# Modulation dots cut into pieces and begun at the gate tiles, and a bank of their own for the opening's idle products

## The chip, the cores and the metric

One core of one Trainium2 chip runs the whole kernel. The metric is device time in microseconds (us) of one execution; lower is better. TensorE (PE) multiplies into PSUM, its weight loads are shown as PEld; VectorE (DVE) and ScalarE (ACT) do the elementwise work; GpSimd (POOL) and SyncE (SP) mostly issue transfers here.

## The reference

Two layers, each over x of 512 tokens by 1024 features. A vector c of 1024 numbers steers each layer through six modulation vectors:

```
c_act = silu(c)
mod = c_act @ w_ada + b_ada                 # 1024 -> 6 * 1024
sh1, sc1, g1, sh2, sc2, g2 = split(mod, 6)
h = rmsnorm(x, norm1_w) * (1 + sc1) + sh1
u = h @ w_in                                # pool, conv, q, k, v and three gates per feature
merged = sum over the three mixers of sigmoid(gate_i) * (mixer_i @ p_i)
x = x + g1 * (merged @ w_out)
h2 = rmsnorm(x, norm2_w) * (1 + sc2) + sh2
x = x + g2 * ((silu(h2 @ w_gate) * (h2 @ w_up)) @ w_down)
```

The third mixer is block-sparse causal attention with eight heads of 64. All values are fp32.

## The kernel before

Activations lie with features on the 128 partitions and the 512 tokens along the free dimension, in eight tiles. Each fp32 product is made of three products of rounded halves (`mm3`, line 155): high by high, high by low, low by high. Weights come in tiles of eight 128x128 blocks. `load_w` fetches one into a buffer of the tag `raw`, of which there are three, and splits it: ScalarE copies the high half (`whi`), and the low half (`wlo`) is made either by VectorE (line 402) or, for most input columns and for the attention tiles, by ScalarE and an accumulating transfer (lines 419, 421 and 423). `next_w` hands them out in order and loads three or four ahead.

The modulation vectors are not computed on TensorE. For each of the six parts and each of its eight tiles of 128 features, `ada_load` fetches 128 rows of the transposed w_ada, and `ada_dot` (line 479) multiplies them by silu(c), laid out on all partitions as `csil`, and sums along the free dimension: one VectorE instruction over 128x1024 that leaves one column of `mod`. `ada_end` adds the bias and, for a scale, folds in the norm's weight.

These dots are spread between the products by a queue, `bulk`. `mm3` counts columns, and every 2048 of them (four calls, twelve products) is a tick. A tick steps the attention's generators and gives the queue a credit, `bulk_rate`. As long as the credit is not negative the next task is emitted and its cost subtracted. Unused credit is kept up to 4.0, and `flush_bulk` emits all that is left. Emission sets the place in the program; VectorE's dots keep that order.

In layer 0 the parts are placed so. The first scale and shift (`SC1`, `SH1`) are computed in the opening with the first norm. The second scale (`SC2`) is queued when the attention has begun, with `early` set: its tiles use the `raw` buffers, since the others are in use by the attention, and the load of the next tile is emitted ahead of each dot. The first gate (`G1`) and the second shift (`SH2`) follow at the first attention tile of the merge, the step `("attn", 0)` of the list `GATE2`, and the second gate (`G2`) at the output projection:

```
if l == 0:
    bulk.extend(ada_tasks(l, (SC2,), True))
bulk_rate[0] = 0.0
ahead_now[0] = 3
ready.append(gate())
...
    if j == 2:
        bulk_rate[0] = 0.25
```

Here the merge of pool and convolution branches runs over j, two gate tiles and four products for each, while the attention of four head pairs runs in between. Then come the third gate and the attention branch by `GATE2`, and the output projection in `tail`, which flushes the queue ahead of its sixth column and prepares the second norm.

In the opening, the squares of x are summed over the features by products with two columns of ones, into bank 0 of the two-bank tile `scratch`. Products of `ones` by `ones`, which nobody reads, go to bank 1 (`idle`): three of them after the sums and five after the root of the norm has been spread by four transposes. Each is two MATMULs in the trace. The root is read from bank 0 by ScalarE (line 920).

Of the kernel before, what the change touches and what calls it, by code (L numbers as in the profile page):

```python
# [17 lines left out]
ALU = mybir.AluOpType  # L18
AX = mybir.AxisListType
PSUM = bass.MemoryType.PSUM  # L20

P = 128
D = 1024
S = 512
L = 2
KT = D // P
# [37 lines left out]
SH1, SC1, G1, SH2, SC2, G2 = range(6)  # L64
# [9 lines left out]

WARM = 9

WARM2 = (3, 5)

GATE2 = ([("gate", j) for j in range(6)] + [("attn", 0), ("attn", 1), ("gate", 6), ("gate", 7)]
         + [("attn", j) for j in range(2, 8)])  # L80
# [3 lines left out]
def hybrid_trunk(ctx, tc, xT, ws, ada, cols, pool_w, qk_w, crow, pos, con, out):  # L84
    nc = tc.nc
    V, A, T = nc.vector, nc.scalar, nc.tensor
# [10 lines left out]
    def nm(s):  # L97
        uid[0] += 1
        return f"{s}{uid[0]}"
# [7 lines left out]
    def ps_mm():  # L107
        return psum.tile([P, S], F32, tag="mm", name=nm("mm"), bufs=4)

    def ps_pair():  # L110
        return psum.tile([P, 2, S], F32, tag="pair", name=nm("pair"), bufs=2)

    def w4(shape, dt=F32):
        return work.tile(shape, dt, tag="w4", name=nm("w4"), bufs=6)

    def sm(shape, dt=F32, tag="sm", bufs=8):
        return small.tile(shape, dt, tag=tag, name=nm(tag), bufs=bufs)
# [7 lines left out]
    bulk = deque()  # L125
    bulk_rate, credit = [0.0], [0.0]
# [8 lines left out]
    def flush_bulk():  # L135
        while bulk:
            bulk.popleft()[1]()
# [12 lines left out]
    def drain():  # L150
        while fibers:
            tick()

    def matmul(*a, **k):
        tc.keep_in_program_order(T.matmul(*a, **k))  # L155

    def pin(ins):
        return tc.keep_in_program_order(ins)

    def transpose(*a):  # L160
        tc.keep_in_program_order(T.transpose(*a))  # L161
# [28 lines left out]
    csil = const.tile([P, D], F32, name="csil")  # L190

    c8, ccol = sm([KT, P], tag="c8", bufs=1), sm([P, KT], tag="ccol", bufs=1)
# [13 lines left out]
    ones = f32(ones_r)  # L206
# [70 lines left out]
    class GateUp:  # L277
# [9 lines left out]
        def load(self, sub):  # L287
            if sub < 2:
                return self.pair[sub].first()
            if sub < 6:  # L290
                return self.pair[sub % 2].sums(sub // 2 - 1)
            raw = rawt()
            fetch(raw, self.l, self.pair[0].blocks(1, 1) + self.pair[1].blocks(1, 1))
            return split_w(raw, C_BLOCKS)
# [159 lines left out]
    def next_w(ahead=None):  # L454
        ahead = ahead_now[0] if ahead is None else ahead
        while at[0] < len(items) and len(loaded) <= ahead:
            loaded.append(load_w())
        return loaded.popleft()

    def wblk(w, b):  # L460
        return w[0][:, b, :], w[1][:, b, :]
# [6 lines left out]
    mod = [const.tile([P, 6, KT], F32, name=f"mod{l}") for l in range(L)]  # L468
    amod = [[const.tile([P, KT], F32, name=f"am{l}{i}") for i in range(2)] for l in range(L)]

    def fold_scale(l, i, j0, j1):
        part = SC1 if i == 0 else SC2
        nw = colt[:, l, (C_N1 if i == 0 else C_N2) + j0:(C_N1 if i == 0 else C_N2) + j1]
        V.scalar_tensor_tensor(amod[l][i][:, j0:j1], mod[l][:, part, j0:j1], 1.0, nw,
                               op0=ALU.add, op1=ALU.mult)
# [9 lines left out]
    def ada_first_load(j, after=None, parts=(SC1, SH1)):  # L485
        tiles = {}
        for part in parts:
            tiles[part] = w4([P, D])
            with issued_after(after):
                nc.sync.dma_start(tiles[part], ada[0, part, j])  # L490
        return tiles
# [7 lines left out]
    def ada_first(j, tiles, part):  # L499
        first_dots[j, part] = pin(ada_dot(tiles[part], 0, part, j))  # L500
        m = mod[0][:, part, j:j + 1]
        if part == SC1:
            ins = A.activation(amod[0][0][:, j:j + 1], m, AF.Identity, scale=minus[:, j:j + 1],
                               bias=abias[:, j:j + 1])
        else:
            ins = A.activation(m, m, AF.Identity, bias=colt[:, 0, C_ADA + part * KT + j:C_ADA + part * KT + j + 1])
        if j == 0:

            pin(ins)
        return ins  # L510

    def ada_load(l, part, j, early, kept):
        aw = wp.tile([P, D], F32, tag="raw", name=nm("raw"), bufs=RAW) if early else w4([P, D])
        nc.sync.dma_start(aw, ada[l, part, j])
        kept.append(aw)

    def ada_step(l, part, j, kept):
        aw = kept.pop(0)
        with tc.issue_after(dots_after[0].ins) if dots_after[0] is not None else nullcontext():
            ins = ada_dot(aw, l, part, j)  # L520
        pin(ins)

    def ada_end(l, part):
        m = mod[l][:, part]
        V.tensor_add(m, m, colt[:, l, C_ADA + part * KT:C_ADA + (part + 1) * KT])
        if part in (SC1, SC2):
            fold_scale(l, 0 if part == SC1 else 1, 0, KT)
        if part == G1:
            V.tensor_scalar(m, m, 0.5, None, op0=ALU.mult)

    def ada_tasks(l, parts, early=False):
        every = [(part, j) for part in parts for j in range(KT)]
        kept, out = [], []
        load = lambda n: ada_load(l, *every[n], early, kept)

        def step(n):
            if early and n + 1 < len(every):
                load(n + 1)
            if not early:
                load(n)  # L540
            ada_step(l, *every[n], kept)

        if early:
            out.append((1.2, lambda: load(0)))
        for n, (part, j) in enumerate(every):
            out.append((1.2, lambda n=n: step(n)))
            if j == KT - 1:
                out.append((0.2, lambda part=part: ada_end(l, part)))
        return out
# [323 lines left out]
    scratch = ps_pair()  # L873
# [3 lines left out]
    for i in range(WARM):  # L877
# [4 lines left out]
        if i == 6:  # L882
            for j in range(KT):
# [4 lines left out]
    step = []  # L888
    pin(V.tensor_scalar(minus, colt[:, 0, C_N1:C_N1 + KT], -1.0, None, op0=ALU.mult))
    pin(V.scalar_tensor_tensor(abias, colt[:, 0, C_ADA + SC1 * KT:C_ADA + (SC1 + 1) * KT], 1.0,  # L890
                               minus, op0=ALU.add, op1=ALU.mult))
# [3 lines left out]
    def sum_tokens(t):  # L895
# [2 lines left out]
                   start=not groups and i == 0, stop=len(groups) == KT // 2 - 1, skip_group_check=True)  # L898
        groups.append(t)

    def idle(n):
        for _ in range(n):
            matmul(scratch[:, 1, :P], ones, ones, start=True, stop=True)

    for k in range(KT):
        if k == 0 or (k % 2 == 1 and k < KT - 1):
# [9 lines left out]
    first[0].update(ada_first_load(0, step[3], (SH1,)))  # L916
    idle(WARM2[0])
    ss = scratch[:, 0, :2 * TT].rearrange("p (t c) -> p t c", c=2)[:, :, 0]
# [7 lines left out]
    for i in range(TT):  # L926
        transpose(norm.rstd[:, i * P:(i + 1) * P], r[:, i:i + 1].to_broadcast([P, P]), ident)
    idle(WARM2[1])
    ada_first(0, first[0], SH1)
    norm.first_scaled(0)  # L930
# [21 lines left out]
    for l in range(L):  # L952
# [230 lines left out]
        for t, src in keys_values(qk, ss, made, tables, turn):  # L1183
            for half in range(2):
                part = src[:, half * BLOCK:(half + 1) * BLOCK].rearrange("p (n d) -> p n d", d=HD)
# [5 lines left out]
        def gate():  # L1191
            g = ps_mm()
            feature_tile(g, next_w())
            sg = bigt(F32)
            A.activation(sg, g, AF.Tanh, scale=0.5)
            return sg
# [18 lines left out]
            y_pool.append(split_from(pp, scale=col(C_PS + j)))  # L1215

        if l == 0:
            bulk.extend(ada_tasks(l, (SC2,), True))
        bulk_rate[0] = 0.0
        ahead_now[0] = 3  # L1220
        ready.append(gate())

        def gated(sg, branch):

            V.scalar_tensor_tensor(sg, sg, 1.0, branch, op0=ALU.add, op1=ALU.mult)

        pcw = None
        for j in range(KT):
            s0, s1 = [ready.pop(0) if ready else gate() for _ in range(2)]
            if j == 2:  # L1230
                bulk_rate[0] = 0.25
            if j % 2 == 0:
                pcw = next_w()
            b0 = 4 * (j % 2)
            p1, p2 = ps_mm(), ps_mm()
            for z in range(2):
                mm3(p1, wblk(pcw, b0 + z), y_pool[z], z == 0, z == 1)
            for z in range(2):
                mm3(p2, wblk(pcw, b0 + 2 + z), y_conv[z], z == 0, z == 1)
            gated(s0, p1)  # L1240
            gated(s1, p2)
            V.tensor_add(s0, s0, s1)
            m01.append(s0)
# [4 lines left out]
        for step, j in GATE2:  # L1248
            if step == "gate":
                sg2[j] = gate()  # L1250
                continue
            if j == 0:
                drain()
                flush_bulk()
                if l == 0:
                    bulk.extend(ada_tasks(l, (SH2,)))
                late = len(bulk)
                bulk.extendleft(reversed(ada_tasks(l, (G1,))))
                bulk_rate[0] = 0.95 if l == 0 else 1.3
                if l == 0:  # L1260
                    credit[0] = 0.0
            if j % 2 == 0:
                aw_ = next_w()
            p1 = ps_mm()
            for z in range(PAIRS):
                mm3(p1, wblk(aw_, 4 * (j % 2) + z), y_attn[z], z == 0, z == PAIRS - 1)
            t = sg2.pop(j)
            gated(t, p1)
            V.tensor_add(t, t, m01[j])  # L1269
            merged.append(split_from(t))  # L1270
# [159 lines left out]
        for part, (along, single, pairs) in enumerate(PARTS):  # L1430
# [28 lines left out]
            if l + 1 < L:  # L1459
                if part == 0:  # L1460
                    later = ada_tasks(l + 1, (SC1, SH1, SC2, SH2))
                n = DOTS[part]
# [14 lines left out]
            else:  # L1477
# [7 lines left out]
                scratch = ps_pair()  # L1485
# [103 lines left out]
```

## Time and profile before

| | |
|---|---|
| median of 3 runs | 1437.39 us (1436.78 to 1439.01) |
| the profiled execution | 1437.1 us |
| its span, first to last instruction | 1435.3 us |
| PE busy | 1426.4 us (99%) |
| DVE busy | 1042.7 us (73%) |
| ACT busy | 765.3 us (53%) |
| POOL busy | 179.5 us (13%) |
| mean granted clock of TensorE | 0.996 of 2.4 GHz |

A busy TensorE is not one at its peak, since the ends of its pipelined products are modelled; waits show better in stretches that do the same work. Times in the rows below count from the span's start. In a row of the timeline the two first numbers are start and length, and a bracket at the end tells how long the engine was idle before it and what ended that.

### The profile page before, as it was taken

The page shows a single profiled execution, that of the slowest core. Times are in us where ns is not written, and L with a number is a line of the kernel's source. Part 1 is how long each engine was busy: PE and PEld are TensorE (multiplying, and loading weights), DVE is VectorE, ACT ScalarE, POOL GpSimd, SP SyncE. Part 2 cuts the span into 40 slices and gives each one's busy share as a digit, 9 for nine tenths or more (in the row PEclk, how much of TensorE's full clock was granted, in tenths as well). Part 3 has the DMA queues.
Part 4 walks back from the last instruction along what each step waited for, and adds up shares of the span by engine and source line. Part 5 has one row for each costly group of instructions (what it writes and reads, how often), then busy time and mean ns, then how long its engine had stood idle before and what let it go on. Part 6 is the DMA issues. An engine that isn't in the chain of part 4 may idle for free.

```text
span 1435.3 us, 22123 instructions
## 1 busy us (share of the span) xinstructions
PE 1426.4 (99%) x8304; PEld 1256.2 (88%) x8304; DVE 1042.7 (73%) x1929; ACT 765.3 (53%) x1275; POOL 179.5 (13%) x246
## 2 busy tenths in 40 slices
PE   9999999999999999999999999999999999999999
PEld 8888888887988998989998888888889989999997
DVE  7899766559886867667788986665778747657663
ACT  5777666743553452535454676667336525435450
POOL 0111111100200210211001111111020102111200
PEclk8999999999999999999999999999999999999999
DMA  9878777797636766747527676767872537646522
GB/s 340 246 198 216 192 178 176 172 318 247 162 128 218 194 177 205 191 133 206 199 88 243 170 194 140 158 160 186 302 211 81 144 106 185 171 113 179 140 85 85
DMA packets 96587, 259.67 MB, mean 181 GB/s; under 512 B 12248, under 2 KB 24928, under 8 KB 96480
## 3 DMA queue, kind: packets, MB, share of 16 engines
q1 hardware_dynamic: 67312, 177.37, 36.1%
q0 software_dynamic: 28576, 80.76, 28.3%
q8 instruction: 65, 1.06, 0.3%
q14 instruction: 42, 0.34, 0.1%
q10 hardware_dynamic: 592, 0.14, 0.0%
HBM read 256.12 MB, written 2.10 MB: 180 GB/s over the span
## 4 chain that ended last, share of the span: by engine, by line
PE 91%; DVE 3%; DMA 2%; ACT 2%; issue 1%; POOL 0%; ACTq 0%; DVEq 0%; POOLq 0%
PE mm L155 78%; PE pair L155 12%; PE mm L161 2%; DMA raw<-in_ws 1%; DVE w L479 1%; DVE wlo L402 1%; DMA wlo<-in_ws 1%; ACT whi L419 0%; DVE tmp L658 0%; DVE big L665 0%; ACT wlo L421 0%; ACT big L676 0%; DVE big L677 0%; DMA w<-in_ada 0%; DVE big L1269 0%
## 5 line engine op out<-in xcount | busy, mean ns | idle before, releaser
L155 PE MATMUL mm<-big,whi 128*128 128x512 f32 (+1 forms) x4334 | 1073.5, 339 | 0.8 <-ACT big L676 0.6
L155 PEld LDWEIGHTS mm<-big,whi 128*128 128x128 f32 x4334 | 741.5, 190 | 87.3 <-issue 2.2
L155 PE MATMUL mm<-big,wlo 128*128 128x512 f32 (+1 forms) x2167 | 732.2, 338 | 0.2
L155 PEld LDWEIGHTS mm<-big,wlo 128*128 128x128 f32 x2167 | 411.1, 190 | 45.3 <-issue 0.9
L399 ACT ACTIVATE whi<-raw 128x1024 fp32r<-128x1024 f32 (+2 forms) x170 | 174.4, 1028 | 158.5 <-PE mm L155 88.2
L402 DVE TENSOR_TENSOR wlo<-raw,whi 128x1024 fp32r<-128x1024 f32 (+2 forms) x170 | 199.1, 1181 | 42.3 <-ACT whi L399 41.8
L399 ACT ACTIVATE whi<-w 128x1024 fp32r<-128x1024 f32 x84 | 88.9, 1058 | 155.2 <-PE mm L155 89.4
L402 DVE TENSOR_TENSOR wlo<-w,whi 128x1024 fp32r<-128x1024 f32 x84 | 101.2, 1220 | 28.6 <-ACT whi L399 27.9
L479 DVE SCALAR_TENSOR_TENSOR w<-w,csil 128x1024 f32<-128x1024 f32 x88 | 105.2, 1219 | 14.2 <-DMA w<-in_ada 14.2
L1276 DVE SCALAR_TENSOR_TENSOR x<-mm,mod,x 128x512 f32<-128x512 f32 (+1 forms) x89 | 61.4, 693 | 69.8 <-PE mm L155 69.5
L423 POOL DMA_DIRECT2D wlo<-in_ws x66 | 56.8, 861 | 404.8 <-ACT wlo L421 285.7
L261 POOL DMA_DIRECT2D w<-in_ws x72 | 47.8, 688 | 440.2 <-DVE wlo L402 155.3
L419 ACT ACTIVATE whi<-raw 128x1024 fp32r<-128x1024 f32 x66 | 70.1, 1063 | 46.7 <-PE mm L155 32.4
L263 POOL DMA_DIRECT2D w<-in_ws x72 | 64.6, 919 | 149.8 <-DMA w<-in_ws 142.0
L155 PE MATMUL pair<-whi,big 128*128 128x512 f32 x256 | 83.2, 390 | 0.0
L155 PE MATMUL pair<-big,whi 128*128 128x256 f32 (+1 forms) x392 | 78.9, 298 | 0.0
L421 ACT ACTIVATE wlo<-whi 128x1024 fp32r<-128x1024 f32 x66 | 69.3, 1055 | 0.6
L155 PEld LDWEIGHTS pair<-big,whi 128*128 128x128 f32 x392 | 63.4, 191 | 2.8
L155 PE MATMUL pair<-big,wlo 128*128 128x256 f32 (+1 forms) x196 | 58.4, 298 | 0.0
L155 PEld LDWEIGHTS pair<-whi,big 128*128 128x128 f32 x256 | 48.3, 189 | 9.9
L676 ACT ACTIVATE big<-big 128x512 fp32r<-128x512 f32 x52 | 32.5, 627 | 40.4 <-DVE big L1269 18.8
L677 DVE TENSOR_TENSOR big<-tmp,big 128x512 fp32r<-128x512 f32 x48 | 33.0, 690 | 26.2 <-ACT big L676 25.2
(236 smaller groups left out, 1421.7 us busy)
## 6 DMA issues: line engine op xcount, KB each, us to landing
raw<-in_ws SPq DMA_DIRECT2D x146, 512.0 KB, 4.3
w<-in_ada SPq DMA_DIRECT2D x88, 512.0 KB, 5.6
w<-in_ws POOLq DMA_DIRECT2D x144, 256.0 KB, 4.5
wlo<-in_ws POOLq DMA_DIRECT2D x66, 512.0 KB, 7.1
raw<-in_ws SPq DMA_DIRECT2D x64, 256.0 KB, 4.1
raw<-in_ws SPq DMA_DIRECT2D x24, 384.0 KB, 3.6
raw<-in_ws SPq DMA_DIRECT2D x16, 448.0 KB, 5.1
raw<-in_ws SPq DMA_DIRECT2D x36, 128.0 KB, 3.0
```

What stands on the lines that cost most here:

```text
L155: tc.keep_in_program_order(T.matmul(*a, **k))
L261: nc.gpsimd.dma_start(dst, self.source(0, 1))
L263: nc.gpsimd.dma_start(dst, self.source(*other), accum_op=ALU.add)
L399: A.activation(hi[:, :n], raw[:, :n], AF.Copy)
L402: ins = V.tensor_sub(lo[:, :n], raw[:, :n], f32(hi)[:, :n])
L419: A.activation(hi[:, :n], raw[:, :n], AF.Copy)
L421: A.activation(lo[:, :n], f32(hi)[:, :n], AF.Copy, scale=-1.0)
L423: nc.gpsimd.dma_start(lo[:, i:i + m].rearrange("p b n -> p (b n)"), src, accum_op=ALU.add)
L479: return V.scalar_tensor_tensor(aw, aw, 1.0, csil, op0=ALU.mult, op1=ALU.mult, accum_out=mod[l][:, part, j:j + 1])
L676: A.activation(hi, src, AF.Copy)
L677: last_split[0] = V.tensor_sub(lo, src, f32(hi))
L1276: V.scalar_tensor_tensor(x[k][:, lo:hi], src, mod[l][:, part, k:k + 1], x[k][:, lo:hi], op0=ALU.mult, op1=ALU.add)
```

## The change

The second scale's and the first gate's dots of layer 0 are cut into four instructions of 256 columns each, which leave four partial sums; at the end of a part one reduction adds them. Both parts are queued where the second scale was, one piece at a time, with a cost of 0.35 and a rate of 0.36 from the first tick on, and the credit starts at -0.35 instead of what was left over. The tile of the next dot is loaded with the first piece of a dot. The pieces of the gate that are left at the first attention tile are not flushed: they run on at the rate of that stage (0.95), and the second shift's dots are queued behind them. The credit of -0.35 also holds for layer 1, where the queue is empty at that point. In the opening the idle products get a single bank of their own and are two and eight instead of three and five.

```
-WARM2 = (3, 5)
+WARM2 = (2, 8)
...
+    PIECES = 4
+
+    def ada_pieces(l, part):
+
+        sums = sm([P, P], tag="c8", bufs=1)[:, part % 2 * KT * PIECES:][:, :KT * PIECES].rearrange("p (j i) -> p j i", i=PIECES)
+        kept, n = [], D // PIECES
+
+        def step(j, i):
+            if i == 0 and j + 1 < KT:
+                ada_load(l, part, j + 1, True, kept)
+            c = slice(i * n, (i + 1) * n)
+            aw = kept[0]
+            pin(V.scalar_tensor_tensor(aw[:, c], aw[:, c], 1.0, csil[:, c], op0=ALU.mult, op1=ALU.mult,
+                                       accum_out=sums[:, j, i:i + 1]))
+            if i == PIECES - 1:
+                kept.pop(0)
+
+        def end():
+            V.tensor_reduce(mod[l][:, part], sums, axis=AX.X, op=ALU.add)
+            ada_end(l, part)
+
+        out = [(0.35, lambda: ada_load(l, part, 0, True, kept))]
+        out += [(0.35, lambda j=j, i=i: step(j, i)) for j in range(KT) for i in range(PIECES)]
+        return out + [(0.35, end)]
...
+    spare = ps_mm()
+
     def idle(n):
         for _ in range(n):
-            matmul(scratch[:, 1, :P], ones, ones, start=True, stop=True)
+            matmul(spare[:, :P], ones, ones, start=True, stop=True)
...
         if l == 0:
-            bulk.extend(ada_tasks(l, (SC2,), True))
-        bulk_rate[0] = 0.0
+            bulk.extend(ada_pieces(l, SC2) + ada_pieces(l, G1))
+        bulk_rate[0], credit[0] = 0.36 if l == 0 else 0.0, -0.35
...
-            if j == 2:
-                bulk_rate[0] = 0.25
...
             if j == 0:
                 drain()
-                flush_bulk()
                 if l == 0:
+                    late = 9
                     bulk.extend(ada_tasks(l, (SH2,)))
-                late = len(bulk)
-                bulk.extendleft(reversed(ada_tasks(l, (G1,))))
+                else:
+                    flush_bulk()
+                    late = len(bulk)
+                    bulk.extendleft(reversed(ada_tasks(l, (G1,))))
                 bulk_rate[0] = 0.95 if l == 0 else 1.3
```

## Rows read from the trace of the kernel before

**Rows 1.** Stretches (us) of layers 0 and 1: length, busy us by engine.

```profile
core 0: us, PE busy (x) PEld busy (x) DVE busy (x) ACT busy (x) POOL busy (x), PEclk, DMA share, GB/s
137.81:179.34 41.53, 41.10 (x217) 33.78 (x217) 32.24 (x87) 26.65 (x58) 5.17 (x6) 1.00 0.80 203
179.34:220.04 40.70, 40.70 (x218) 33.88 (x217) 26.83 (x76) 27.36 (x57) 4.85 (x6) 1.00 0.68 170
220.04:261.70 41.66, 41.16 (x218) 33.89 (x217) 27.79 (x81) 27.43 (x58) 5.17 (x7) 1.00 0.79 184
...
887.60:928.30 40.70, 40.70 (x218) 33.88 (x217) 24.16 (x72) 27.45 (x58) 4.87 (x6) 1.00 0.61 142
...
290.19:376.40 86.21, 84.97 (x404) 70.59 (x404) 67.33 (x113) 32.45 (x45) 9.09 (x14) 1.00 0.84 271
997.49:1081.00 83.51, 83.51 (x404) 70.60 (x404) 59.68 (x96) 32.22 (x45) 11.75 (x16) 1.00 0.80 246
```

**Rows 2.** Timeline of the opening, TensorE and ScalarE.

```profile
9.54 3.24 PE L155 MATMUL pair<-ones,big 128*128 128x2 f32 x16 [0.35 <-DVE big L914]
12.64 1.63 PE L155 MATMUL pair<-ones 128*128 128x128 f32 x6
14.37 0.26 ACT L920 ACTIVATE root<-pair,epst 128x4 f32<-128x4 f32 x1 [4.73 <-PE pair L155]
18.18 0.77 PE L155 MATMUL mm<-whi,big 128*128 128x512 f32 x1
20.81 0.39 PE L155 MATMUL pair<-wlo,big 128*128 128x512 f32 x1
```

**Rows 3.** Timeline of the opening, TensorE's weight loads.

```profile
15.98 2.26 PEld L155 LDWEIGHTS pair<-ones 128*128 128x128 f32 x10
```

**Rows 4.** Stretches of the opening: PE busy, granted clock (1.00 is 2.4 GHz), DMA.

```profile
15.50:20.00 4.50, 4.50 (x18) 0.50 1.03 410
20.00:20.50 0.50, 0.50 (x3) 0.82 1.04 417
```

**Rows 5.** Timeline at the start of layer 0's gate tiles.

```profile
149.29 1.22 DVE L479 SCALAR_TENSOR_TENSOR raw<-raw,csil 128x1024 f32<-128x1024 f32 x1
150.44 1.22 DVE L479 SCALAR_TENSOR_TENSOR raw<-raw,csil 128x1024 f32<-128x1024 f32 x1
154.90 1.06 ACT L419 ACTIVATE whi<-raw 128x1024 fp32r<-128x1024 f32 x1 [1.62 <-DMA raw<-in_ws]
```

**Rows 6.** Timeline: a dot's load on SyncE's queue; end of a later dot.

```profile
173.04 0.33 SPq L514 DMA_DIRECT2D raw<-in_ada  x1
...
236.06 0.08 DVE L479 DVE_READ_ACCUMULATOR raw<-raw,csil 128x1 f32 x1
```

**Rows 7.** Timeline of ScalarE in the third head pair.

```profile
229.59 1.06 ACT L419 ACTIVATE whi<-raw 128x1024 fp32r<-128x1024 f32 x1 [2.38 <-DMA raw<-in_ws]
```

**Rows 8.** Line 419 from 147 to 320 us, and what it waited for.

```profile
L419 ACT ACTIVATE whi<-raw x25: 1044/1061/1094, 154.9 to 306.0; 128x1024 fp32r<-128x1024 f32 x25
...
  DMA raw<-in_ws: 6.6, 4
```

**Rows 9.** Timeline from the third attention tile to the output projection's first column.

```profile
319.79 0.69 DVE L1225 SCALAR_TENSOR_TENSOR big<-big,mm 128x512 f32<-128x512 f32 x1 [3.94 <-PE mm L155]
...
337.94 0.40 PE L155 MATMUL mm<-big,wlo 128*128 128x512 f32 x1
...
339.63 0.50 PE L155 MATMUL mm<-big,whi 128*128 128x512 f32 x1 [0.22 <-DVE big L677]
```

**Rows 10.** Timeline at the end of the output projection.

```profile
369.08 1.22 DVE L479 SCALAR_TENSOR_TENSOR w<-w,csil 128x1024 f32<-128x1024 f32 x1
...
376.02 0.39 PE L155 MATMUL pair<-big,ones 128*128 128x256 f32 x1 [0.37 <-DVE big L613]
```

**Rows 11.** Timeline of VectorE, operations of 256 columns back to back.

```profile
70.41 0.42 DVE L1007 TENSOR_TENSOR big<-big 128x256 f32<-128x256 f32 x1
70.75 0.42 DVE L1008 SCALAR_TENSOR_TENSOR big<-big,big 128x256 f32<-128x256 f32 x1
```

**Rows 12.** The chain of waits: a run of 24 products of 512 columns.

```profile
160.07 5.47 PE mm L155 x24
```

## The prediction, on record before the changed kernel ran

> **What bounds the kernel now.** I read the page first: TensorE is busy for 99% of the span, so only the places where it waits can give time. A busy share does not show these well, so I cut the trace into stretches that do the same products in both layers. Layer 1 has no dots beside its attention and serves as the measure. One head pair takes 40.70 us there. Layer 0 takes 41.53, 40.70 and 41.66 for its first three, so 0.83 and 0.96 us are lost. From the last attention tile to the second norm, layer 0 takes 86.21 us and layer 1 83.51: 2.70 us more [rows 1]. Everything that the dots cost in layer 0's first half is thus 0.83 + 0.96 + 2.70 = 4.5 us. The fourth place is the opening.
>
> **Opening.** The sixteen sums end at 12.78 us, but the root on ScalarE starts only at 14.37, just after the three idle products that follow them end at 14.27 (12.64 + 1.63). Root and idle products touch different banks of one tile, so the root waits for products that it does not read. The first real product starts at 18.18 and the eighth at 20.81 [rows 2]. The ten weight loads of the second idle group run from 15.98 for 2.26 us, so they end where the first real product begins [rows 3]. The clock is 1.2 GHz until 20 us and back at 2.4 GHz soon after [rows 4].
>
> **The change, part by part.**
>
> *Idle products.* With their own bank the root can start at about 12.88, 1.49 us earlier, and the rest of that chain with it (three small VectorE steps, the transposes, the first scaled tile). The two idle products that stay ahead of the transposes last 2/3 of 1.63 us, to about 13.7, and the transposes come at 15.28 - 1.49, about 13.8 (15.28 is where they start today): they hide there. But eight idle products are sixteen weight loads at 0.226 us, 3.62 us. From 15.98 - 1.49 = 14.49 they last to 18.11, and only 0.07 us would be left. That is the low end, 0.1 us: idle products then take the place of the wait. The high end is the whole shift, 1.5 us. Which end is nearer hangs on the clock. Today TensorE stops from 14.27 to about 15.3 and the clock comes back 4.2 us after 15.98. In the new order it works from 12.6 to 18.1 with breaks of 0.1 or 0.2 us, so I expect the clock back some two us earlier, the last idle products shorter, and the first real ones at full rate. I take 0.9 us. All eight first products at full rate would be worth 20.81 - 18.18 - 7 x 0.228 = 1.0 us [rows 2, 12], which I leave to a rival. The new tile is the fourth of four single banks there; two of the others were emptied long before, so nothing waits for a bank.
>
> *The burst of three dots goes.* Today the credit left over from earlier lets three whole dots out at the first tick, 1.15 us each from start to start, some 3.4 us of VectorE in one piece. Their tiles also occupy all three raw buffers until then, and ScalarE waits 1.62 us for the first weight tile behind them [rows 5]. The head pair with this burst loses 0.83 us [rows 1]. The new credit of -0.35 lets out one task per tick (12 products, 2.7 us). Ends 0 and 0.83; I take 0.6, because the raw wait disappears with the burst.
>
> *Two raw tiles held, longer.* A dot in four pieces holds its tile for four ticks, and the next one is loaded at its first piece. So two of three raw buffers are taken from 147 us until the gate's last piece, near 310. Today two are held from the load at 173.04, which goes out ahead of the dot on the tile before it, to the dot that ends at 236.1 [rows 6]. Weights then pass through one buffer, and a ScalarE copy that stands in line for a tile not landed yet blocks what is behind it: it waited 2.38 us at 229.59 [rows 7], in the stretch that lost 0.96. Yet 179 to 220 us runs under the same condition and loses nothing [rows 1]. Ends: +0.96, if no copy waits because the loads are more even; and -1.5, if 163 us under this condition cost at the rate of today's 63 (0.96 x 163/63 = 2.5, less 0.96). I take -0.4, near today's stretches.
>
> *Four of the gate's eight dots move.* By counting the tasks against the credit tick by tick, 47 of the 68 are out before the first attention tile of the merge: the scale's 34, and three of the gate's dots with the load. The other 21 need 21 x 0.35 / 0.95 = 7.7 ticks, where today eight dots need 9.8/0.95 = 10.3. So the second shift's dots start three ticks earlier. Between the third and the last attention tile the new order issues as many dots as today (about five), so VectorE is as crowded there. The wait behind it, from 337.94 to 339.63 less two products, 1.2 us, should stay: its last link is a split behind a table load. VectorE is idle 3.94 us ahead of the third tile [rows 9], which covers pieces that wait for their loads; without this cover they would add to the 1.2. Zero, ends -1.2 and +1.2.
>
> *The rest of the shift and second gate.* Today two shift dots are out when the out projection starts and fourteen remain. Ten leave by the ticks; four are flushed at once, the last at 369.08, and the norm's sum waits for VectorE at 376.02 [rows 10]. With four out earlier, two are flushed, 2.3 us less VectorE just ahead of that wait. The ends are 0 and what is left of the 2.70 us, 1.5; I take 1.0.
>
> *More VectorE work.* A 256-wide operation of this kind is 0.42 us long and starts 0.34 after the one ahead [rows 11]. With the accumulator's read I take 0.36, so four pieces are 1.43 against 1.15. Sixteen dots cost 4.5 us more, twelve of them in the attention, where VectorE is busy about 28 of 41 us [rows 1]: hidden by its idle third; uncovered, 4.5 us. [...]
>
> Layer 1 gets the credit of -0.35 too, so its four first gate dots leave one at a time. Its TensorE is busy for all of 83.51 us [rows 1], so I count nothing. The two reductions of the sums have 128 x 32 elements and lie off the path: nothing.
>
> **Sum.** 0.9 + 0.6 - 0.4 + 0 + 1.0 = 2.1 us. The profiled execution took 1437.1 us (span 1435.3 and 1.8 around it), 0.3 below the median of 1437.39. So 1435.0 on its basis, 1435.3 as a median.
>
> **Rivals.**
>
> *Weights starve (slower).* The 25 copies of this kind from 147 to 320 us wait four times for a load, 6.6 us together [rows 8], while TensorE loses 0.83 + 0.96 = 1.79: 0.45 us per waiting tile. With one raw buffer all along, 18 waiting tiles lose 8.0 us. Less the 1.79 of today and the 1.9 of opening and projection this is 4.3 us slower, 1441.7. It is over 0.2% from about 15 tiles on. For it: two tiles held for 163 us. Against it: 179 to 220 us loses nothing.
>
> *All of it goes through.* Opening 1.5, burst 0.8, raw waits 0.9, projection 1.4: 4.6 us, 1432.8. For it: layer 1 without a single wait. Against it: the raw buffers. The clock's 1.0 would come on top.
>
> *It doesn't do what it says.* The idle products end where the wait ended (0.1), attention trades one wait for another (0), only the projection gains a little (0.4): 1436.9.
>
> **How the numbers follow.** 0.2% is 2.9 us, about what a measurement here can tell from no change. Forecast 45% (its own range 1434.0 to 1436.6), all through 28%, does nothing 15%, starvation 12%. Faster by over 0.2% holds most of the second case and the forecast's lower edge: 34%. Slower holds two thirds of the last: 8%. Within: 58%. The range goes from 1432.0 to 1439.4 and leaves out the best of the second case with the clock's gain, and the worse half of starvation.
>
> **What would show it.** Root near 12.9 us, first real product before 17.8, clock back before 19; if the idle products end at 18.1, the low end holds. Head pairs of layer 0 near 40.7 to 41.3; more than 42 means that the one raw buffer costs, and ScalarE's copies then wait for their loads. Two dots flushed ahead of 369 us and the norm's sum without a wait. The 1.2 us ahead of the out projection still there. The forecast fails if the copies wait in most tiles, or if nearly every layer 0 wait vanishes.

## The result, and the profile after

The changed kernel takes 1449.85 us (median of 5 runs, 1447.97 to 1449.99) where the kernel before takes 1437.39: a ratio of 1.0079, 95% interval 1.0068 to 1.0090. It is slower by 0.8%. The forecast was 1435.3 us with a range of 1432.0 to 1439.4, so the time lies outside it, on the side that had been given 8%. The profiled execution has a span of 1446.6 us, 11.3 above before.

First the stretches of [rows 1], cut at the same products, in the windows of the changed kernel (length; busy us of each engine with its count of instructions; granted clock, DMA share, GB/s):

```profile
137.75:178.45 40.70, 40.70 (x218) 33.88 (x217) 31.83 (x97) 26.39 (x58) 5.17 (x6) 1.00 0.65 160
178.45:219.91 41.46, 41.03 (x218) 34.07 (x217) 28.02 (x96) 25.81 (x56) 4.31 (x5) 1.00 0.70 177
219.91:260.63 40.72, 40.72 (x218) 33.81 (x217) 28.47 (x97) 29.32 (x59) 5.71 (x7) 1.00 0.83 213
289.58:387.71 98.13, 88.92 (x404) 73.10 (x404) 66.77 (x145) 34.14 (x47) 10.38 (x14) 0.95 0.80 242
```

The three head pairs together take 122.88 us, 1.01 less than before. The fourth pair loses 0.46 of it again (28.95 against 28.49 us), so at 289.58 the changed kernel is 0.61 us ahead. The whole loss lies in the fourth row, from the last attention tile to the second norm: 98.13 against 86.21 us for the same 404 products. TensorE's idle time there grows from 1.24 to 9.21 us, and its busy time by 3.95 us with a granted clock of 0.95. So the 11.9 us are 8.0 us of added waiting and 3.95 us of longer products, which go with the lower clock behind the waits. All of TensorE's waits in the fourth row:

```profile
303.86 0.82 PE L155 MATMUL mm<-big,whi 128*128 128x512 f32 x2 [1.70 <-ACT big L876]
328.63 0.80 PE L155 MATMUL mm<-big,wlo 128*128 128x512 f32 x1 [4.20 <-DMA wlo<-in_ws]
346.58 0.50 PE L155 MATMUL mm<-big,whi 128*128 128x512 f32 x1 [0.68 <-DVE big L702]
349.71 0.50 PE L155 MATMUL mm<-big,whi 128*128 128x512 f32 x1 [2.40 <-ACT big L701]
350.44 0.77 PE L155 MATMUL mm<-big,whi 128*128 128x512 f32 x1 [0.23 <-DVE big L702]
```

The windows of TensorE show waiting and clock at the largest place, and the clock behind the last three waits:

```profile
322.00:324.00 2.00, 2.00 (x10) 1.00 0.86 227
324.00:326.00 2.00, 0.43 (x2) 1.00 0.98 246
326.00:328.00 2.00, 0.00 (x0) 0.65 1.05 299
328.00:330.00 2.00, 1.37 (x3) 0.50 1.09 270
330.00:332.00 2.00, 2.00 (x6) 0.50 0.82 176
332.00:334.00 2.00, 2.00 (x7) 0.64 0.80 281
334.00:336.00 2.00, 2.00 (x11) 1.00 0.45 180
...
350.00:352.00 2.00, 1.77 (x5) 0.62 0.43 170
352.00:354.00 2.00, 2.00 (x7) 0.52 0.72 246
```

TensorE stands still for 4.2 us, the granted clock falls to 0.50 of its full rate (the traces give the clock only as such a share; the 1.2 GHz of the prediction stands for the same 0.50), and until 333 us the next products go more slowly (6 or 7 in two us, not 10 or 11). From 350 to 354 us it is low once more (0.62 and 0.52). The wait that ends at 328.63 is for the low half of a weight tile, which could be made only behind ScalarE's copy at 322.25, and this copy had waited for its load. Line 419 from 147 to 360 us (its last copy starts at 322.2; in [rows 8] it was 306.0), then ScalarE's waiting copies from 285 us in the timeline, the waited time in brackets:

```profile
L419 ACT ACTIVATE whi<-raw x24: 1046/1061/1089, 150.8 to 322.2; 128x1024 fp32r<-128x1024 f32 x24
...
  DMA raw<-in_ws: 26.8, 13
```

```profile
295.32 1.06 ACT L419 ACTIVATE whi<-raw 128x1024 fp32r<-128x1024 f32 x1 [5.06 <-DMA raw<-in_ws]
299.86 1.06 ACT L419 ACTIVATE whi<-raw 128x1024 fp32r<-128x1024 f32 x1 [1.85 <-DMA raw<-in_ws]
317.54 1.06 ACT L419 ACTIVATE whi<-raw 128x1024 fp32r<-128x1024 f32 x1 [5.23 <-DMA raw<-in_ws]
322.25 1.06 ACT L419 ACTIVATE whi<-raw 128x1024 fp32r<-128x1024 f32 x1 [2.08 <-DMA raw<-in_ws]
328.18 1.06 ACT L399 ACTIVATE whi<-raw 128x1024 fp32r<-128x1024 f32 x1 [3.29 <-DMA raw<-in_ws]
```

Why the loads come late is seen in SyncE's queue (timeline, from 285 us on; line 239 loads weights, line 514 the tiles of dots: the gate's into `raw`, those of the second shift into `w4`):

```profile
286.48 0.33 SPq L514 DMA_DIRECT2D raw<-in_ada  x1
287.53 0.33 SPq L239 DMA_DIRECT2D raw<-in_ws  x1
287.91 0.42 SPq L514 DMA_DIRECT2D w<-in_ada  x1
296.40 0.33 SPq L239 DMA_DIRECT2D raw<-in_ws  x1
296.78 0.90 SPq L514 DMA_DIRECT2D w<-in_ada  x2
300.95 0.33 SPq L514 DMA_DIRECT2D raw<-in_ada  x1
301.32 1.31 SPq L514 DMA_DIRECT2D w<-in_ada  x2
304.85 0.33 SPq L514 DMA_DIRECT2D raw<-in_ada  x1
305.29 0.42 SPq L514 DMA_DIRECT2D w<-in_ada  x1
308.95 0.33 SPq L239 DMA_DIRECT2D raw<-in_ws  x1
```

Only three weight tiles are ordered between 287 and 309 us. The issue at 296.40 comes right behind the copy that starts at 295.32 (295.32 + 1.06 = 296.38), the one at 300.95 behind the copy of 299.86: these loads wait for the copy ahead to free a buffer, and each copy waits for its load. The issue at 308.95 comes right behind one of the gate's pieces, which frees its tile then (308.50 + 0.42 = 308.92). A tile's load takes 3.6 us in the attention and twice that here, by the issues of line 239 first from 240 to 285, then from 285 to 325 us:

```profile
DMA to landing us min/median/max: 3.1/3.6/5.7
```

```profile
DMA to landing us min/median/max: 3.6/7.2/7.8
```

By these medians, as an estimate, one buffer brings a tile every 7.2 + 1.06 = 8.3 us, where a tile of 24 products is used up in 5.47 [rows 12]; in the attention 3.6 + 1.06 = 4.7 was just enough. It is a lower bound: the weights were ordered 8.87 and 12.55 us apart, with two of the gate's tiles in the queue ahead of the last one. The gate's pieces (line 543) wait as well, which holds their tiles longer still (timeline of VectorE; the gate's last piece comes at 331.1, not near 310):

```profile
308.50 0.42 DVE L543 SCALAR_TENSOR_TENSOR raw<-raw,csil 128x256 f32<-128x256 f32 x1
...
318.86 0.43 DVE L543 SCALAR_TENSOR_TENSOR raw<-raw,csil 128x256 f32<-128x256 f32 x1 [2.39 <-DMA raw<-in_ada]
324.21 0.42 DVE L543 SCALAR_TENSOR_TENSOR raw<-raw,csil 128x256 f32<-128x256 f32 x1 [3.88 <-DMA raw<-in_ada]
329.26 1.22 DVE L402 TENSOR_TENSOR wlo<-raw,whi 128x1024 fp32r<-128x1024 f32 x1 [4.63 <-ACT whi L399]
```

The last waits, at 346 to 350 us, end on the splits of the merged tiles and not on weights. The chain that ended last leads from them almost without a break through VectorE's work, which had piled up, back to a weight load. A tile of the gate stands on it before:

```profile
300.95 7.97 DMA raw<-in_ada
...
320.36 7.80 DMA raw<-in_ws
```

### The profile page after: what moved, and what is told of

The parts are those of the page before. It is cut to its first block, busy times and chain, and to the rows that moved or that the text cites. A ratio compares the mean times of both kernels' runs of the same rounds, so it can differ in the third digit from the quotient of the medians.

```text
span 1446.6 us, 22227 instructions
## 1 busy us (share of the span) xinstructions
PE 1430.3 (99%) x8308; PEld 1259.5 (87%) x8308; DVE 1047.2 (72%) x2027; ACT 765.7 (53%) x1275; POOL 179.5 (12%) x246
## 3 DMA queue, kind: packets, MB, share of 16 engines
q8 instruction: 65, 1.06, 0.3%
## 4 chain that ended last, share of the span: by engine, by line
PE 85%; DVE 6%; DMA 5%; ACT 2%; issue 1%; SPq 0%; DVEq 0%; ACTq 0%
PE mm L155 73%; PE pair L155 10%; DMA raw<-in_ws 3%; PE mm L161 1%; DMA wlo<-in_ws 1%; DVE w L479 1%; DVE wlo L402 1%; DMA raw<-in_ada 1%; ACT whi L419 0%; DVE raw L543 0%; DMA x<-in_xT 0%; DVE big L1252 0%; DVE tmp L683 0%; DVE big L690 0%; DVE big L702 0%
## 5 line engine op out<-in xcount | busy, mean ns | idle before, releaser
L479 DVE SCALAR_TENSOR_TENSOR w<-w,csil 128x1024 f32<-128x1024 f32 x80 | 95.6, 1218 | 15.6 <-DMA w<-in_ada 15.5
L155 PE MATMUL pair<-wlo,big 128*128 128x512 f32 x128 | 50.0, 390 | 0.5 <-DMA wlo<-in_ws 0.5
```

Of the source, the lines that this page charges most:

```text
L479: return V.scalar_tensor_tensor(aw, aw, 1.0, csil, op0=ALU.mult, op1=ALU.mult, accum_out=mod[l][:, part, j:j + 1])
```

## The experiments

Theory: the gate's tiles in `raw` leave weights too few buffers (buffer theory). Rivals: VectorE (64 pieces and an earlier second shift crowd the splits), the transfers themselves, the opening. Each edit is against the changed kernel, unless it says otherwise; each kernel ran beside the kernel before on one chip, so the ratios are compared. Dots mark what is left out of an edit.

**e1, the gate's tiles in other buffers.**

```diff
-    def ada_pieces(l, part):
+    def ada_pieces(l, part, early=True):
...
-                ada_load(l, part, j + 1, True, kept)
+                ada_load(l, part, j + 1, early, kept)
...
-            bulk.extend(ada_pieces(l, SC2) + ada_pieces(l, G1))
+            bulk.extend(ada_pieces(l, SC2) + ada_pieces(l, G1, False))
```

> The first gate's tiles of layer 0 lie in the six buffers for moment tiles and dots (w4) instead of the three raw ones; pieces, rates, order and transfers stay. Buffer theory (from 290 us on the gate's dots and the weight tiles pass in turn through three raw buffers, and the in-order load queue stands still behind each tile that waits for one): the 11.3 us between 290 and 390 us come back, about 1438, and ScalarE's copies there wait for a load four times or fewer. VectorE theory (sixteen dots in 64 pieces and an earlier second shift crowd the splits): still about 1450. Transfer theory (the same bytes, moved earlier, are too much for the DMA engines in that stretch): still about 1450.

Measured 1434.65 us, ratio 0.9985 (0.9975 to 0.9995): the loss is gone, with the same pieces, ticks and bytes. That answers the rivals of VectorE's work and of the bytes: both are all there. Line 399 no longer waits for a load after 285 us; TensorE in the windows of e1, where the changed kernel had 5.80 and a clock of 0.83:

```profile
320.00:330.00 10.00, 10.00 (x46) 1.00 0.50 188
330.00:340.00 10.00, 9.16 (x40) 1.00 0.48 161
```

**e2, thin pieces.**

```diff
-            c = slice(i * n, (i + 1) * n)
+            c = slice(i * n, i * n + (n if part == SC2 else 32))
```

> Each piece of the first gate multiplies 32 of its 256 columns (the rest of its sum is left out), so VectorE's work for these 32 pieces falls by some 0.25 us each, 8 us in all; the tiles are loaded and held as in the changed kernel. Buffer theory: the tiles are still held, so 1447 to 1450. VectorE theory: the work is gone, about 1438 to 1441. Transfer theory: 1450.

Measured 1446.70, ratio 1.0065 (1.0046 to 1.0085). A thin piece takes 0.18 us instead of 0.42, so more than half of the gate's time on VectorE is out, and nearly all of the loss stays: VectorE's work is not the cause.

**e3, pieces without loads.**

```diff
-            if i == 0 and j + 1 < KT:
+            if i == 0 and j + 1 < KT and part == SC2:
...
+            if part == G1:
+                pin(V.scalar_tensor_tensor(dump, csil[:, c], 1.0, csil[:, c], op0=ALU.mult, op1=ALU.mult,
+                                           accum_out=sums[:, j, i:i + 1]))
+                return
...
-        out = [(0.35, lambda: ada_load(l, part, 0, True, kept))]
+        out = [(0.35, lambda: part == SC2 and ada_load(l, part, 0, True, kept))]
```

> The first gate's eight tiles are not loaded: its pieces multiply the conditioning row by itself at full width into a small tile (so the gate's values are left out), and no raw buffer is held for them; one large tile fewer pays for the small one. Buffer theory: about 1436 to 1438. Transfer theory: the same, since 4 MB are not moved; e1 tells these two apart. VectorE theory: the 32 pieces are all there, about 1448 to 1450.

Measured 1435.45, ratio 0.9990 (0.9981 to 1.0000). All the work on VectorE, no load of the gate and no tile held: no loss.

**e4, the second scale in pieces, the gate as before** (the diff's last part, at the first attention tile, undone).

```diff
-            bulk.extend(ada_pieces(l, SC2) + ada_pieces(l, G1))
+            bulk.extend(ada_pieces(l, SC2))
```

> Only the second scale's dots are in pieces from the gate tiles on; the first gate's are whole, from the first attention tile of the merge, as in the kernel before; the opening is the changed one. All three theories put the loss on the gate's dots, so 1435 to 1438, the two raw tiles being held only up to about 236 us; the gain of the first head pair (0.83 us) stays. If the second scale's pieces themselves cost, 1440 or more.

Measured 1435.81, ratio 0.9986 (0.9977 to 0.9995): this half of the change gains a little, and the gate's half holds the whole loss.

**e5 and e6, a fourth raw buffer, in the changed kernel and in the kernel before.**

```diff
-RAW, BIG = 3, 46
+RAW, BIG = 4, 44
```

> The changed kernel with four raw buffers; 44 large tiles instead of 46 pay for the fourth. Buffer theory: two weight tiles are under way where one was, so most of the 12.5 us comes back: 1435 to 1440, and the copies in the merge wait for a load six times or fewer. If a different wait holds the weights (the order on VectorE, the transfers themselves): 1448 to 1451.

> Control for e5: the kernel before with four raw and 44 large buffers. If the two large tiles are not missed, 1435 to 1438; what it lies above 1437.4 is the price of the smaller pool and is to be taken off e5.

Measured 1449.27, ratio 1.0078 (1.0061 to 1.0096), and 1441.05, ratio 1.0026 (1.0016 to 1.0036). The two large tiles are missed. Against its control e5 is slower by 0.52%, 7.5 us: a fourth buffer gives back some 5 of 12.5 us, not most. The expectation of the buffer theory failed in its size. In e5 the copies of lines 419 and 399 from 285 us on still wait five times for a load, 16.0 us, against 18.7 in the changed kernel.

**e7, whole dots in the places of the pieces.**

```diff
-            bulk.extend(ada_pieces(l, SC2) + ada_pieces(l, G1))
+            bulk.extend([(1.4, f) if c > 1 else (c, f) for c, f in ada_tasks(l, (SC2, G1), True)])
```

> The changed kernel with whole dots of 1024 columns at 1.4 credit each in place of four pieces at 0.35: the same places, rates, tiles and transfers, 4.5 us less on VectorE. The tile of a dot is freed by one instruction, yet it is taken as early as before. Buffer theory: about as slow as the changed kernel, 1446 to 1452. If it is the pieces (their number or their waits in VectorE's order): 1436 to 1440.

Measured 1441.92, ratio 1.0034 (1.0022 to 1.0046): between the two. A whole dot frees its tile at once and orders the next load with it; a tile in pieces stays for four ticks beside the next one. So the pieces do matter. That it is by how long they hold fits this, but e7 also takes out work and waits of VectorE and doesn't part them.

**e8, faster pieces.**

```diff
-        bulk_rate[0], credit[0] = 0.36 if l == 0 else 0.0, -0.35
+        bulk_rate[0], credit[0] = 0.56 if l == 0 else 0.0, -0.35
```

> The rate of the pieces from the gate tiles on is 0.56 instead of 0.36, so all 68 tasks should be out before the first attention tile of the merge, and no raw buffer is held by a dot from about 280 us on; tiles and buffers stay. Buffer theory, with the merge as its place: the 290 to 390 us loss goes and the attention pays a little for faster dots: 1435 to 1440. If holding two raw buffers anywhere costs about the same per microsecond, it is as slow as the changed kernel, 1446 or more.

Measured 1452.39, ratio 1.0102 (1.0085 to 1.0119), the slowest of all. The merge is not the place as such: the loss went with the loads. Nor does the sum of load and copy foretell it: the landing median of line 239 is 5.1 us from 240 to 285, which makes 6.2 us against 5.47, 0.7 short for a tile; yet the five weight tiles of that stretch were ordered 9.0 us apart on average (244.5 to 280.5), and TensorE is idle for 12.1 us from 180 to 300. In the windows of e8 TensorE now waits in the attention, and from 310 us no more; line 419 waits 15 times, 37.5 us.

```profile
190.00:200.00 10.00, 7.55 (x30) 0.83 0.93 212
250.00:260.00 10.00, 6.74 (x37) 1.00 0.62 152
290.00:300.00 10.00, 6.03 (x28) 0.84 0.58 152
```

**e11, the second shift's dots behind the merge.**

```diff
-                    late = 9
-                    bulk.extend(ada_tasks(l, (SH2,)))
+                    late = 0
...
         while len(bulk) > late:
             bulk.popleft()[1]()
+        if l == 0:
+            bulk.extend(ada_tasks(l, (SH2,)))
```

> The changed kernel, but the second shift's eight dots are put in the list only behind the last attention tile of the merge (the gate's remaining pieces are all issued there too), so no dot of it stands between the splits of 330 to 350 us; raw tiles as in the changed kernel. Buffer theory, in which the weights come late whatever VectorE does: 1445 or more. If the second half of the loss is VectorE catching up with the shift's dots (five or six at 1.14 us on the chain from 329 to 350): 1441 to 1444, and part of that lost again in the out projection.

Measured 1448.20, ratio 1.0075 (1.0058 to 1.0093). The shift's dots stand on the chain of waits after 329 us, and taking them off gives nothing that can be measured. The waits at 346 to 350 us (3.3 us) are gone from its trace, but new ones of 1.6 us together stand between 380 and 390 at a lower clock (0.83), so e11 does not show that these dots cost nothing.

**e13 and e14, buffers held by nothing.** To e1 is added, with one and with two tiles (shown with two):

```diff
+            def hold_raw():
+                for _ in range(2):
+                    kept_raw.append(rawt())
+                    pin(V.memset(kept_raw[-1][:, 0, :1], 0.0))
+            def free_raw():
+                for t in kept_raw:
+                    pin(V.tensor_copy(t[:, 0, 1:2], t[:, 0, :1]))
-            bulk.extend(ada_pieces(l, SC2) + ada_pieces(l, G1, False))
+            bulk.extend(ada_pieces(l, SC2) + [(0.0, hold_raw)] + ada_pieces(l, G1, False) + [(0.0, free_raw)])
```

> e1 (the gate's tiles in w4), and one raw buffer taken by two operations of one column each, from the gate's first piece to its last, with nothing else in it: two of three are left for weights. Buffers alone: 4 to 8 us above e1, 1439 to 1443, as e5 and e7 with two left. If it is the dots' own place in the queues: 1434 to 1436, as e1.

> The same with two raw buffers taken, one left for weights. Buffers alone: 10 us or more above e1, 1445 or more, since then a copy must end before the next load starts, and a load takes 3 to 8 us where the merge wants a tile every 3.5 us or so. If it is the dots' own place in the queues: under 1440.

Measured 1437.57, ratio 1.0004 (0.9991 to 1.0016), and 1443.85, ratio 1.0049 (1.0032 to 1.0066). With three, two and one buffer for weights the ratio is 0.9985, 1.0004 and 1.0049: the first buffer costs about 2.7 us (less than expected, and the intervals of e1 and e13 just overlap), the second 6.5 more (0.45%); with 1443.85 us e14 too stays short of the 1445 expected. The 3.5 us that its expectation gives for a tile in the merge is not what is measured: 24 products take 5.47 [rows 12]. Buffers held by nothing thus cost 0.64%, 9.2 us, of the 0.94%, 13.5 us, by which the changed kernel lies above e1. TensorE's idle time in e14 falls from 330 to 350 us (6.7 us), later than in the changed kernel. Line 419 of e14, with no dot in any raw tile from 266 to 323 us:

```profile
L419 ACT ACTIVATE whi<-raw x24: 1045/1060/1095, 150.7 to 313.6; 128x1024 fp32r<-128x1024 f32 x24
...
  DMA raw<-in_ws: 28.6, 15
```

**e15, loads without holding.**

```diff
+        dump = sm([P, n], tag="dump", bufs=1)
...
-            pin(V.scalar_tensor_tensor(aw[:, c], aw[:, c], 1.0, csil[:, c], op0=ALU.mult, op1=ALU.mult,
+            o, a = (dump, csil[:, c]) if part == G1 else (aw[:, c], aw[:, c])
+            pin(V.scalar_tensor_tensor(o, a, 1.0, csil[:, c], op0=ALU.mult, op1=ALU.mult,
                                        accum_out=sums[:, j, i:i + 1]))
```

> The changed kernel, but the first gate's pieces multiply the conditioning row by itself into a small tile (the gate's values are left out), so that its eight tiles are loaded into raw buffers and freed when they have landed, with no piece waiting for them; one large tile fewer. If the loads' passage through raw buffers and queue is most of the rest: 1441 or more. If the holding by waiting pieces is: 1435 to 1439.

Measured 1439.02, ratio 1.0009 (0.9990 to 1.0028). The eight loads pass through the same buffers and queue, and most of the loss is gone, so the passage alone is not the cause. Two things are out at once, the holding by the pieces and the pieces' waits for their tiles; of these, e14 has the holding alone. The ten times lie in two groups, five from 1436.2 to 1437.1 and five from 1441.0 to 1447.6 us, so the median stands for neither, and the passage can't be priced (0.24% above e1, 3.4 us, by the middle).

**e9 and e10, the opening alone, and with fewer idle products** (in the kernel before; the edit of e9, with `WARM2 = (2, 5)` in e10).

```diff
-WARM2 = (3, 5)
+WARM2 = (2, 8)
...
+    spare = ps_mm()
...
-            matmul(scratch[:, 1, :P], ones, ones, start=True, stop=True)
+            matmul(spare[:, :P], ones, ones, start=True, stop=True)
```

> The kernel before with the opening's part of the change alone: idle products in a bank of their own, two ahead of the transposes and eight behind. Prediction's low end, which the changed trace shows: root some 0.9 us earlier, first real product no earlier because sixteen idle weight loads fill the gap; 1437.2, within 0.1% of the kernel before. If the opening caused part of the loss, 1440 or more.

> The same bank, with two and five idle products: ten weight loads behind the transposes, about 2.3 us, which end near 17.3 us, when the first scaled tile is ready too. If the gain of the shorter chain was only covered by idle products: first real product near 17.3, and up to 0.9 us of it in the time, 1436.5. If the products behind it wait for weights and rows anyway: first product early, but level with the kernel before by 85 us, 1437.2.

Measured 1436.23, ratio 0.9992 (0.9982 to 1.0002), and 1436.67, ratio 0.9988 (0.9979 to 0.9996): the opening costs nothing and may be worth a us or so; e9 can't be told from no change. Its trace went another way than the changed kernel's: the clock was back (1.00 from 15.5 us) before the idle products ended (16.31). TensorE's timeline in e9:

```profile
13.46 2.85 PE L155 MATMUL mm<-ones 128*128 128x128 f32 x16
16.07 0.47 PE L155 MATMUL mm<-whi,big 128*128 128x512 f32 x1
```

In e10 the first real product waits for ScalarE's first scaled tile and not for idle products:

```profile
17.25 0.50 PE L155 MATMUL mm<-whi,big 128*128 128x512 f32 x1 [0.18 <-ACT big L662]
```

A transposition that stands at 126.41 us in the kernel before stands at 124.76 in e9 and 124.87 in e10, so the lead is not lost by 85 us, as e10's second expectation had it. An earlier clock goes with it: 1.00 from 15.5 us in e9 and from 16.5 in e10, from 20.5 in the kernel before; how much of the lead that makes is not shown.

**e12, e1 with five idle products.**

```diff
-WARM2 = (2, 8)
+WARM2 = (2, 5)
```

> e1 (the gate's tiles in w4) with two and five idle products. If the opening's gain lasts, 0.5 to 0.9 us below e1; if not, the same as e1, 1434.0 to 1435.0. Both below the kernel before.

Measured 1433.42, ratio 0.9973 (0.9962 to 0.9984): faster than the kernel before by 3.9 us and than the changed one by some 15. That it beats e1 is not shown, as their intervals overlap.

## Why the prediction was wrong, point by point

- **Two raw tiles held, longer: -0.4 us, ends +0.96 and -1.5. This step failed.** It is the term that was mis-sized: the merge lost 11.9 us, and the holding alone costs 9.2 by e14 against e1. It priced 163 us of holding by the 63 us in the head pairs, where a load lands in 3.6 us. The holding was now to reach into the merge, where a load takes 7.2: there one buffer falls short of TensorE, by 8.3 us against 5.47. The landing times of the kernel before would have warned of it: 3.2 us from 240 to 285, 10.6 from 285 to 325 us (medians of line 239), with a DMA share of 0.96 in the second. That the landing time sets the size is argued from this sum and not shown; e8, which lost more with the gate's pieces pulled into the attention, speaks against it as the whole account. With the gate's tiles elsewhere e1 lies 0.15%, 2.2 us (0.7 to 3.6), below the kernel before, and the other terms of the sum made 2.5: nothing here contradicts the rest of the prediction in its total.
- **The rival "weights starve"** had the right mechanism and the wrong price. It counted 18 waiting tiles at 0.45 us and came to 1441.7. Line 419 waited 13 times, for 26.8 us, and the stage paid 11.9. Its rate came from stretches where 6.6 us of waiting cost 1.79, the rest costing TensorE nothing; in the changed kernel, too, 10.1 us of such waits from 150 to 240 us go with 0.43 us of idle time in its three head pairs. In the merge 18.7 us of waiting from 285 us on (14.2 on line 419, 4.5 on line 399) stand against 8.0 us of idle time, and half as much again (3.95) goes with the clock.
- **Four dots moved: 0, ends ±1.2.** The count was near: ten of the gate's pieces are out at 300 us and fifteen at 305.8, when the first attention tile of the merge is gated; twelve were counted. The cover of 3.94 us on VectorE [rows 9] was no cover, since the weights behind waited for the same buffers. What was named there as the risk happened: the idle time ahead of the output projection grew from 0.79 us (0.57 and 0.22, the second in [rows 9]) to 3.31, beyond the lower end.
- **The burst: +0.6.** The first head pair went from 41.53 to 40.70 us, all of the 0.83. The third gained 0.94, the second lost 0.76.
- **Opening: +0.9.** In the profiled execution it was the low end: root at 13.48 us, idle weight loads from 15.08 to 18.61, first real product at 18.57, later than the 18.18 before; the clock is back at about 19.4, and the eighth comes 0.15 earlier than in [rows 2]. e9 puts it at 0.08% (-0.02 to 0.18), 1.1 us: the term itself was not wrong, but one execution does not show it.
- **Rest of the shift: +1.0.** The norm's sum runs without a wait (387.04, four products in a row), which is worth the 0.37 us of [rows 10], and no more of this term is shown; the last dots come in pairs at 372 and 376.67.
- **VectorE: hidden.** The 64 pieces have a median of 0.419 us and start 0.345 apart back to back, where the prediction took 0.36; a whole dot takes 1.22 (1.15 from start to start, [rows 5]). By e1, e2 and e3 this work is not what costs.

What stays open: by the ratios, the changed kernel lies 0.30% (4.3 us) above e14, which holds as many buffers. The gate's loads in the queue and the waits of the pieces on VectorE are the candidates; no run parts them, and e15 spreads too widely to price the first. Both intervals together leave room from about 1.5 to 7 us.

## What to carry to other kernels

Cutting work into small pieces spread over ticks makes its operands live longer; count the buffer time (tile times ticks held), not the instructions. Whether the buffers left are enough is one sum for each stage: load time plus copy, over the buffers left, against the time in which TensorE uses a tile up, with the landing time of that very stage. The sum is a first test and no forecast of the loss: in e8 it came out 0.7 us short for a tile where the tiles were ordered 9.0 us apart. If it falls short, move the tiles to another pool before touching rates: here that turned +0.8% into -0.15%.

## What the runs showed of the hardware

- Waiting cost TensorE more here than the wait: an idle stretch from 324.4 to 328.6 us was followed by a granted clock of 0.50 from 328 to 333, and the 3.3 us of waits from 345.9 to 350.4 by a granted clock of 0.62 and 0.52 from 350 to 354. The shorter wait of 1.70 us that ended at 303.86 was followed by no fall (granted clock 1.00 up to 306). In the stage, 8.0 us of added idle time came with 3.95 us of added busy time for the same 404 products.
- The clock's return in the opening differs from run to run with the same code up to there: with two and eight idle products the granted clock was at 1.00 from about 15.4 us (e4, e9), 16.3 (e1) and 19.4 (the changed kernel), and the first real product came at 16.49, 16.07, 17.34 and 18.57. The rows differ too: in e9 the sums' root starts at 11.65 us, in the changed kernel at 13.48; the granted clock from 11.0 to 11.5 us was 1.00 in the one and 0.50 in the other. So the opening's gain in one trace is not that of its edit alone.
- In one execution of the changed kernel the load of a 128x1024 tile landed in 3.6 us (median from 240 to 285 us) and in 7.2 us (285 to 325). The mean DMA share was 0.83 in both stretches, with 204 and 256 GB/s; what sets the landing time is not shown.
